# Two-pass dense products, later shifted S5 states and inversions in sequence in a hybrid S5 / SSD / DeltaNet layer

## The chip, the cores and the metric

The kernel runs on one core of one Trainium2 chip. The time is the device time of one execution in microseconds (us): the median of three runs before the change is 1144.62 us (1144.04 to 1144.78). One execution was also profiled; all times of single instructions come from it.

The core has a matrix engine (PE, with its weight loads shown apart as PEld), a vector engine (DVE), a scalar engine (ACT), GpSimd (POOL) and SyncE (SP), which here only issues DMAs. Each engine works through its own instructions in the order in which they were written to it; semaphores tie the engines to one another.

## The reference

One inference step of one layer for 384 tokens: 128 context tokens and 256 latent tokens, with D = 1024 channels. Both groups share the weights, and differ in modulation and in where their scans start.

```python
h = _rmsnorm(x, p['norm_g'][0]) * (1.0 + sc1) + sh1
x = x + 0.5 * g1 * _swiglu(h, p['ffn_wi'][0], p['ffn_wo'][0])
h = _rmsnorm(x, p['norm_g'][1]) * (1.0 + sc2) + sh2
mix, states = _mixer_block(h, p, init, grid)
x = x + g2 * mix
h = _rmsnorm(x, p['norm_g'][2]) * (1.0 + sc3) + sh3
x = x + 0.5 * g3 * _swiglu(h, p['ffn_wi'][1], p['ffn_wo'][1])
```

The feed-forward width is 2816. The mixer projects h once (`w_in`) and runs three branches, all in both directions: an S5 diagonal state space model with a gated output, a Mamba-2 SSD scan, and a gated DeltaNet in chunks of 64 tokens, which solves one lower triangular system of 64 rows per chunk, head and direction. The three branch outputs are projected, each is multiplied by the sigmoid of a gate computed from h, and their sum goes through `w_out`. At the end stands a last RMS norm. The outputs are y for both groups and the context's final states.

## The kernel before

**Layout and dense products.** Activations lie with channels on the partitions, in 8 blocks of 128 x 384. Each dense product uses the fp32r form of the matrix engine on split numbers: a value is written as an upper part (the value cast to fp32r) and a lower part (the rest), and the product is upper x upper + upper x lower + lower x upper. `split_w` (L281) gets one weight block ready: SP loads `wraw` (three buffers), ACT casts it to the upper part `whi` (L285), DVE subtracts to give the lower part `wlo` (L286); `whi` and `wlo` have two buffers each. `mm3` (L291) then makes the product of one block into one PSUM tile. For every k it issues three matmuls: `whi` with the upper activation (L294), `whi` with the lower activation (L295), `wlo` with the upper activation (L296). A full block has k = 0..7, so 24 matmuls of 128 x 384; a block of `wbr` has four k and 12 matmuls. Each matmul loads its own weights.

**Stages.** Start and modulation to 50 us; the first feed-forward (`ffn`, FFN 0) to about 345 us, during which DVE also multiplies out the modulation (`ada_rest`, L272) and ACT and DVE make tables for S5; the mixer to about 860 us; the second feed-forward (FFN 1) to 1130 us; the last norm to the end.

**Inside the mixer.** First come the blocks of `w_in` for S5, q, k and v, each followed by a short convolution (`conv`), and for q and k by transposes on PE into a PSUM tile `ps_m` (two buffers), which ACT copies out (`kT`, `qT`, L825). Beside them DVE runs the S5 scan (L830 to L838). `Hc` (L843 to L853) holds the scan's states shifted by one place and is filled by ACT: per part (real, imaginary) eight pieces, small ones that need only constants or the scan's first 16 places, and two large ones (L850, L852). The S5 readout (L979) uses `Hc`. Then the convolutions for the SSD inputs (`xtok`, `bT`, `cT`, `btok`) and the z product (L896 to L898).

**The triangular systems.** `inv16(d)` inverts the 16 x 16 diagonal blocks of all chunks and heads of one direction on DVE, in 15 steps of a product (L953) and a reduction (L955) that depend on each other; it loads its input `U` from `dL` with four DMAs and writes the result (W, and W transposed by POOL, L958) to `dI` with eight DMAs (L961). `inverse(x, d, ps)` then loads `lc`, `Y` and `X` and builds the 64 x 64 inverse by matmuls in `mm64` (L1045). The chunk recurrence of the DeltaNet (`dn_unit`) and the SSD work follow; this sequence is called the chain below.

**Dense work beside the chain.** A generator `gates()` yields after each piece of dense work: the gates (blocks 22 and up of `w_in`) and the first two branch products. `weave` advances several generators in turn, and `every(n, g, steps)` takes one piece of dense work at every n-th turn. After the chain: `og` (the DeltaNet's output gate), br(2) with its sum `mab` (POOL, L1289), then `og` times the normed output `oacc` (L1298), split into `odh` (ACT, L1300) and `odl` (POOL, L1301), br(3), the gated sums, and `w_out`.

**What sets the order.** The code gives a program order, and the scheduler of the tile framework (`schedule_with_timeline_sim=True`) reorders each engine's instructions by its own model of when they are ready. So an edit in one place can move instructions on every engine.

Of the kernel before, what the change touches and what calls it, by code (L numbers as in the profile page):

```python
# [10 lines left out]
F32 = mybir.dt.float32  # L11
# [9 lines left out]
P = 128  # L21
D = 1024
KD = 8
T = 384
# [117 lines left out]
def tile_hybrid(ctx: ExitStack, tc: tile.TileContext, a, o):  # L142
# [148 lines left out]
    def mm3(pt, w, xh, xl, k0, nk, start, stop):  # L291
        hi, lo = w
        for k in range(nk):
            PE.matmul(pt, hi[:, k, :], xh[k0 + k], start=start and k == 0, stop=False)  # L294
            PE.matmul(pt, hi[:, k, :], xl[k0 + k], start=False, stop=False)  # L295
            last_mm[0] = PE.matmul(pt, lo[:, k, :], xh[k0 + k], start=False, stop=stop and k == nk - 1).ins  # L296
# [95 lines left out]
    def ffn(f, xv, hh, hl, fill, rb=None, done=None, early=(), fill2=None):  # L392
# [5 lines left out]
        for part in range(2):  # L398
            gh, gl = blocks("gh", NH, FR), blocks("gl", NH, FR)
            for j in range(NH):  # L400
# [3 lines left out]
                for w, pt in enumerate((pa, pb)):  # L404
                    mm3(pt, early.pop(0) if early else split_w(a["wi"][f, m, w], KD), hh, hl, 0, KD, True, True)
# [22 lines left out]
            for m in range(KD):  # L428
                py = psd.tile([P, T], F32, name="ps_d", tag="ps_d")
                for k0, nk in ((0, 6), (6, 5)):  # L430
                    w = split_w(a["wo"][f, m, :, part * NH + k0:part * NH + k0 + nk], nk)
                    mm3(py, w, gh, gl, k0, nk, k0 == 0, k0 != 0)
# [182 lines left out]
    def dense_in(blk, hh, hl, tw=T, ps=psD):  # L615
        pt = ps([P, tw])
        mm3(pt, split_w(a["win"][blk], KD), hh, hl, 0, KD, True, True)
# [83 lines left out]
    def mixer(es, xv, acc, xh, xl, sc):  # L701
# [139 lines left out]
        nc.sync.dma_start(out=o["s5"], in_=hfin)  # L841
        Hc = []
# [11 lines left out]


        xtok = mp.tile([P, 3, 8, 64], F32, name="xtok")
        for m in range(4):
            raw = conv(wk, next(urs), dense_in(4 + m, hh, hl), m, sv["cb"][:, m:m + 1])
            pt = transposes([raw[:, X3[x]] for x in range(3)])
            S.copy(xtok.rearrange("p x h c -> p x (h c)")[:, :, m * P:m * P + P], pt)  # L860
        bT, cT = mp.tile([P, T], F32, name="bT"), mp.tile([P, T], F32, name="cT")
        conv(wk, next(urs), dense_in(8, hh, hl), 4, sv["cb"][:, 4:5], bT)
        conv(wk, next(urs), dense_in(9, hh, hl), 5, sv["cb"][:, 5:6], cT)
        btok = mp.tile([P, 3, P], F32, name="btok")
        S.copy(btok, transposes([bT[:, X3[x]] for x in range(3)]))
# [140 lines left out]
        def br(n, m, xh, xl):  # L1006
            pt = psd.tile([P, T], F32, name="ps_d", tag="ps_d")
            mm3(pt, split_w(a["wbr"][m, n], 4), xh, xl, 0, 4, True, True)
# [31 lines left out]
        weave(inv16(0), inv16(1), every(3, dense, 5))  # L1040
# [274 lines left out]
        for m in range(KD):  # L1315
# [3 lines left out]
            mm3(py, split_w(a["wout"][m], KD), mgh, mgl, 0, KD, True, True)  # L1319
# [113 lines left out]
```

## Time and profile before

| | value |
|---|---|
| median of three runs | 1144.62 us |
| profiled execution | 1144.53 us |
| span from first to last instruction | 1142.5 us |
| mean granted PE clock, as share of full | 0.987 |
| PE busy | 1090.7 us (95% of the span) |
| PE's weight loads busy | 1025.8 us (90%) |
| DVE busy | 805.2 us (70%) |
| ACT busy | 472.1 us (41%) |
| POOL busy | 145.1 us (13%) |

The span is 2.0 us shorter than the profiled execution's own time. Busy shares are means over stages with different limits: DVE is at 90% or more in parts of FFN 0 and at about half of that in the second feed-forward. "PE busy" counts matmuls whose ends are modelled, at whichever clock was granted. A wait is put down to the semaphore that came last, so the engine named as the releaser is the one whose result was missing, or, where that engine had long been done, something behind it.

### The profile page before, as it was taken

To read this page: it belongs to the slowest core of one execution; us is meant where nothing else is said; L and a number is where in the kernel's file an instruction comes from. 1 tells how busy PE (TensorE), PEld (TensorE's weight loads), DVE (VectorE), ACT (ScalarE), POOL (GpSimd) and SP (SyncE) were. 2 spreads that over 40 slices of the span, in tenths; PEclk is the share of its full clock that TensorE was granted. 3 is DMA by queue.
4 is the path that set the end of the run, shared out by engine and by line. 5 is a ranking of instruction groups with operands and counts; after the bars stand their busy time and mean duration, and the time that the engine had idled before them with its cause. 6 is when DMAs were issued, how large, how long until landed. Compare 5 with 4: busy or idle time off the path is not lost.

```text
span 1142.5 us, 19011 instructions
## 1 busy us (share of the span) xinstructions
PE 1090.7 (95%) x7192; PEld 1025.8 (90%) x7192; DVE 805.2 (70%) x1652; ACT 472.1 (41%) x871; POOL 145.1 (13%) x135
## 2 busy tenths in 40 slices
PE   5999999999899999899899999999999999999996
PEld 2699899999899999799788888999899999999996
DVE  5699988899967759745554567786866974455554
ACT  5354323333355666743333232243444342334341
POOL 0000000000000100036172563116200000000000
PEclk9999999999999999899999999999999999999998
DMA  9787777576574653268646434456745634544342
GB/s 357 281 265 234 226 232 247 178 225 197 147 262 152 158 171 114 74 189 254 182 144 181 116 105 118 141 158 200 247 142 166 205 112 126 147 115 125 106 127 81
DMA packets 106731, 200.29 MB, mean 175 GB/s; under 512 B 34960, under 2 KB 60816, under 8 KB 106384
## 3 DMA queue, kind: packets, MB, share of 16 engines
q1 hardware_dynamic: 104336, 195.94, 55.7%
q10 hardware_dynamic: 2304, 3.15, 0.8%
q8 instruction: 56, 0.92, 0.3%
q14 instruction: 35, 0.29, 0.1%
HBM read 175.56 MB, written 23.49 MB: 174 GB/s over the span
## 4 chain that ended last, share of the span: by engine, by line
PE 78%; DVE 11%; ACT 3%; issue 3%; DMA 3%; SPq 1%; POOL 1%; DVEq 0%; ACTq 0%; POOLq 0%
PE ps_d L296 21%; PE ps_d L294 21%; PE ps_d L295 20%; DVE wlo L286 3%; ACT whi L285 1%; PE ps_s L979 1%; PE ps_c L1045 1%; PE ps_s L789 1%; PE ps_m L876 1%; PE ps_d L244 1%; DVE cv L687 1%; PE ps_s L1045 1%; DMA cb<-in_condr_dram 1%; DMA wraw<-in_wo_dram 1%; PE ps_m L222 1%
## 5 line engine op out<-in xcount | busy, mean ns | idle before, releaser
L285 ACT CAST whi<-wraw 128x1024 fp32r<-128x1024 f32 (+3 forms) x247 | 228.0, 924 | 450.5 <-PE ps_d L295 300.2
L286 DVE TENSOR_TENSOR wlo<-wraw,whi 128x1024 fp32r<-128x1024 f32 (+3 forms) x247 | 275.1, 1114 | 132.2 <-ACT whi L285 130.2
L294 PE MATMUL ps_d<-hh,whi 128*128 128x384 f32 x696 | 239.4, 345 | 9.9 <-ACT whi L285 6.7
L296 PE MATMUL ps_d<-hh,wlo 128*128 128x384 f32 x696 | 240.2, 346 | 1.3 <-DVE wlo L286 1.1
L295 PE MATMUL ps_d<-hl,whi 128*128 128x384 f32 x696 | 238.3, 343 | 0.9 <-DVE hl L382 0.9
L294 PEld LDWEIGHTS ps_d<-hh,whi 128*128 128x128 f32 x696 | 132.1, 190 | 18.8 <-ACT whi L285 9.9
L296 PEld LDWEIGHTS ps_d<-hh,wlo 128*128 128x128 f32 x696 | 132.2, 190 | 7.5 <-DVE wlo L286 4.1
L295 PEld LDWEIGHTS ps_d<-hl,whi 128*128 128x128 f32 x696 | 132.3, 190 | 3.5 <-DVE hl L382 2.2
L296 PE MATMUL ps_d<-gh,wlo 128*128 128x384 f32 x352 | 119.4, 340 | 3.7 <-DVE wlo L286 3.6
L296 PE MATMUL ps_d<-xh,wlo 128*128 128x386 f32 x352 | 119.7, 340 | 0.9 <-DVE wlo L286 0.9
L294 PE MATMUL ps_d<-gh,whi 128*128 128x384 f32 x352 | 119.0, 338 | 1.5 <-ACT whi L285 1.5
L294 PE MATMUL ps_d<-xh,whi 128*128 128x386 f32 x352 | 119.6, 340 | 0.0
L295 PE MATMUL ps_d<-xl,whi 128*128 128x386 f32 x352 | 119.4, 339 | 0.0
L295 PE MATMUL ps_d<-gl,whi 128*128 128x384 f32 x352 | 118.6, 337 | 0.0
L272 DVE SCALAR_TENSOR_TENSOR ajunk<-araw,cb 128x1024 bf16<-128x1024 f32 x80 | 97.4, 1218 | 2.6 <-ACT cb L264 2.6
L296 PEld LDWEIGHTS ps_d<-gh,wlo 128*128 128x128 f32 x352 | 66.0, 188 | 6.4 <-DVE wlo L286 5.6
L294 PEld LDWEIGHTS ps_d<-gh,whi 128*128 128x128 f32 x352 | 66.1, 188 | 2.7 <-ACT whi L285 2.5
L296 PEld LDWEIGHTS ps_d<-xh,wlo 128*128 128x128 f32 x352 | 66.2, 188 | 1.8 <-DVE wlo L286 1.8
L295 PEld LDWEIGHTS ps_d<-xl,whi 128*128 128x128 f32 x352 | 66.6, 189 | 0.0
L294 PEld LDWEIGHTS ps_d<-xh,whi 128*128 128x128 f32 x352 | 66.2, 188 | 0.0
L295 PEld LDWEIGHTS ps_d<-gl,whi 128*128 128x128 f32 x352 | 66.1, 188 | 0.0
L874 POOL TENSOR_TENSOR Atri<-smalls,dahl 128x512 fp32r<-128x512 f32 x36 | 40.8, 1150 | 61.2 <-DVE dahl L772 53.7
(464 smaller groups left out, 1736.2 us busy)
## 6 DMA issues: line engine op xcount, KB each, us to landing
wraw<-in_wi_dram SPq DMA_DIRECT2D x88, 512.0 KB
araw<-in_ada_dram SPq DMA_DIRECT2D x56, 512.0 KB
wraw<-in_win_dram SPq DMA_DIRECT2D x50, 512.0 KB
wraw<-in_wo_dram SPq DMA_DIRECT2D x32, 384.0 KB
wraw<-in_wo_dram SPq DMA_DIRECT2D x32, 320.0 KB
wraw<-in_ada_dram SPq DMA_DIRECT2D x16, 512.0 KB
wraw<-in_wbr_dram SPq DMA_DIRECT2D x32, 256.0 KB
re<-dM SPq DMA_DIRECT2D x24, 192.0 KB
```

What stands on the lines that cost most here:

```text
L222: PE.matmul(pt[32 * g:32 * g + 32, :], c32[:, k, :], raw[:, j, :], start=q < 2, stop=q >= 2, tile_position=(0, 32 * g))
L244: PE.matmul(pt[32 * g:32 * g + 32, :], c32[:, 4 * h + g, :], raw[:, g, :], start=h == 0, stop=h == 1, tile_position=(0, 32 * g))
L272: V.scalar_tensor_tensor(junk, raw, 1.0, cb[:, e], op0=ALU.mult, op1=ALU.mult, accum_out=t[:, b, e:e + 1])
L285: S.copy(hi, raw)
L286: V.tensor_tensor(lo, raw, hi.bitcast(F32), op=ALU.subtract)
L294: PE.matmul(pt, hi[:, k, :], xh[k0 + k], start=start and k == 0, stop=False)
L295: PE.matmul(pt, hi[:, k, :], xl[k0 + k], start=False, stop=False)
L296: last_mm[0] = PE.matmul(pt, lo[:, k, :], xh[k0 + k], start=False, stop=stop and k == nk - 1).ins
L687: V.scalar_tensor_tensor(rows(cv), ur[:, :, tap:tap + 64], w[:, tap:tap + 1], rows(cv), op0=ALU.mult, op1=ALU.add)
L789: PE.matmul(pt[:, ri, g], sw[:, ri, g], UU[:, 4 * b + g], start=True, stop=True)
L874: G.tensor_tensor(A, bc(INCL[d], [P, 4, P], 1), bc(dahl[:, w, x, 12 * d + c0:12 * d + c0 + 4], [P, 4, P], 2), op=ALU.mult)
L1045: PE.matmul(dst[r_, h], lh[r_, h], rh[r_, h] if len(rh.shape) == 3 else rh[r_], start=True, stop=True)
```

## The change

Three edits, made together.

1. `mm3` issues its matmuls in two passes: first all products with `whi` (L297, L298), for every k, then all products with `wlo` (L305). With `late=True` it keeps the old order, with the lower product as L303. That is set for some first blocks of a stage: the first three m of a feed-forward's first part, the second half of the first `wo` block, block 14 of `w_in`, m = 0 of each branch product and of `w_out`.
2. The `Hc` block is written behind the SSD convolutions instead of ahead of them.
3. The two 16 x 16 inversions run one after the other, each woven with three pieces of dense work at every fifth turn, where before both were woven together with five pieces at every third turn.

Line numbers behind `mm3` grow by 9 to 11: the qT copy is L835, the `Hc` pieces L869 to L874, L953/L955/L961 become L963/L965/L971, L1045 becomes L1056, L1298/L1300/L1301 become L1309/L1311/L1312, L1289 becomes L1300.

```diff
-    def mm3(pt, w, xh, xl, k0, nk, start, stop):
+    def mm3(pt, w, xh, xl, k0, nk, start, stop, late=False):
+
+
         hi, lo = w
-        for k in range(nk):
+
+        def upper(k):
             PE.matmul(pt, hi[:, k, :], xh[k0 + k], start=start and k == 0, stop=False)
             PE.matmul(pt, hi[:, k, :], xl[k0 + k], start=False, stop=False)
+
+        for k in range(nk):
+            upper(k)
+            if late:
+                last_mm[0] = PE.matmul(pt, lo[:, k, :], xh[k0 + k], start=False, stop=stop and k == nk - 1).ins
+        for k in range(0 if late else nk):
             last_mm[0] = PE.matmul(pt, lo[:, k, :], xh[k0 + k], start=False, stop=stop and k == nk - 1).ins
...
-                    mm3(pt, early.pop(0) if early else split_w(a["wi"][f, m, w], KD), hh, hl, 0, KD, True, True)
+                    mm3(pt, early.pop(0) if early else split_w(a["wi"][f, m, w], KD), hh, hl, 0, KD, True, True,
+                        late=part == 0 and m < 3)
...
-                    mm3(py, w, gh, gl, k0, nk, k0 == 0, k0 != 0)
+                    mm3(py, w, gh, gl, k0, nk, k0 == 0, k0 != 0, late=m == 0 and k0 > 0)
...
-        mm3(pt, split_w(a["win"][blk], KD), hh, hl, 0, KD, True, True)
+        mm3(pt, split_w(a["win"][blk], KD), hh, hl, 0, KD, True, True, late=blk == 14)
...
         nc.sync.dma_start(out=o["s5"], in_=hfin)
+
+        xtok = mp.tile([P, 3, 8, 64], F32, name="xtok")
...
+        btok = mp.tile([P, 3, P], F32, name="btok")
+        S.copy(btok, transposes([bT[:, X3[x]] for x in range(3)]))
+
         Hc = []
         for ri in range(2):
             hc = big("Hc", (32, 48))
...
             Hc.append(hc)
-
-
-        xtok = mp.tile([P, 3, 8, 64], F32, name="xtok")
...
-        btok = mp.tile([P, 3, P], F32, name="btok")
-        S.copy(btok, transposes([bT[:, X3[x]] for x in range(3)]))
...
-            mm3(pt, split_w(a["wbr"][m, n], 4), xh, xl, 0, 4, True, True)
+            mm3(pt, split_w(a["wbr"][m, n], 4), xh, xl, 0, 4, True, True, late=m == 0)
...
-        weave(inv16(0), inv16(1), every(3, dense, 5))
+        for d in range(2):
+            weave(inv16(d), every(5, dense, 3))
...
-            mm3(py, split_w(a["wout"][m], KD), mgh, mgl, 0, KD, True, True)
+            mm3(py, split_w(a["wout"][m], KD), mgh, mgl, 0, KD, True, True, late=m == 0)
```

The left-out lines of the two moved blocks are unchanged.

**PE around the transposes of q.** `qtok` is q ahead of its transposes, `cv` the convolved SSD input; the number behind `ps_d` names a dense block. Before:

```order
L296 MATMUL ps_d_4905<-hh_3682,wlo_4909 128x384
L695 MATMUL ps_m_4546<-ident_76,qtok_3839 128x128 x4
L695 MATMUL ps_m_4553<-ident_76,qtok_3839 128x128 x4
L695 MATMUL ps_m_4560<-ident_76,qtok_3839 128x128 x4
L695 MATMUL ps_m_4766<-ident_76,cv_4758 128x128 x3
L695 MATMUL ps_m_4810<-ident_76,cv_4802 128x128 x3
L294 MATMUL ps_d_4944<-hh_3681,whi_4947 128x384
L295 MATMUL ps_d_4944<-hl_3683,whi_4947 128x384
```

Now:

```order
L297 MATMUL ps_d_4841<-hh_3682,whi_4844 128x384
L298 MATMUL ps_d_4841<-hl_3684,whi_4844 128x384
L705 MATMUL ps_m_4546<-ident_76,qtok_3839 128x128 x4
L705 MATMUL ps_m_4553<-ident_76,qtok_3839 128x128 x4
L305 MATMUL ps_d_4841<-hh_3681,wlo_4845 128x384 x4
L305 MATMUL ps_d_4841<-hh_3682,wlo_4845 128x384 x4
L297 MATMUL ps_d_4887<-hh_3681,whi_4890 128x384
```

The transposes of q and of `cv` stood in one row between two dense blocks; now two sets of q stand behind the upper pass of a block with its lower pass behind them, and the third set stands 24 matmuls further on, behind the next block's upper pass. On ACT the twelve small `Hc` pieces stand around the three qT copies in both versions; the four large ones, ahead of the next weight cast before, now stand behind the `btok` copy.

**SP's queue around the inversions.** `W_5538` and its three companions are the inversions' results, `U_5537` and the like their inputs. Before:

```order
L948 DMA U_5547<-dL 24x16x16 x4
L283 DMA wraw<-in_win_dram 128x1024 x4
L1317 DMA xo<-dX 128x384 x2
L242 DMA wraw<-in_ada_dram 128x1024 x2
L961 DMA dI<-W_5538 24x16x16 x4
L961 DMA dI<-W_5847 24x16x16 x4
L961 DMA dI<-W_5548 24x16x16 x4
L961 DMA dI<-W_5857 24x16x16 x4
L1051 DMA lc<-dL 128x4x64
L1058 DMA Y<-dI 128x4x64
L1060 DMA X_5893<-dI 128x4x64
```

Now:

```order
L971 DMA dI<-W_5538 24x16x16 x4
L971 DMA dI<-W_5712 24x16x16 x4
L958 DMA U_5722<-dL 24x16x16 x4
L242 DMA wraw<-in_ada_dram 128x1024
L283 DMA wraw<-in_win_dram 128x1024 x4
L242 DMA wraw<-in_ada_dram 128x1024 x2
L971 DMA dI<-W_5723 24x16x16 x4
L971 DMA dI<-W_5891 24x16x16 x4
L1062 DMA lc<-dL 128x4x64
L1069 DMA Y<-dI 128x4x64
L1071 DMA X_5927<-dI 128x4x64
```

The sixteen writes of `dI` stood in one row; now eight stand behind the first inversion, then the second one's loads and seven loads of dense weights, then the other eight. On PE the first matmul of L1045 stood behind 2352 dense matmuls (those of `mm3` and the z product) and now stands behind 2448 of them, which is four blocks of 24.

**PE and POOL at the end of the chain.** The last transposes of `oacc`, and the dense blocks behind them; `ps_d_8491` is the first block of br(3). PE before:

```order
L294 MATMUL ps_d_8225<-hh_3682,whi_8228 128x384
L695 MATMUL ps_s_8010<-ident_76,oacc_5867 128x128 x4
L295 MATMUL ps_d_8225<-hl_3684,whi_8228 128x384
L296 MATMUL ps_d_8225<-hh_3682,wlo_8229 128x384
L294 MATMUL ps_d_8225<-hh_3682,whi_8228 128x384
L295 MATMUL ps_d_8225<-hl_3684,whi_8228 128x384
L296 MATMUL ps_d_8225<-hh_3682,wlo_8229 128x384
L294 MATMUL ps_d_8225<-hh_3682,whi_8228 128x384
L295 MATMUL ps_d_8225<-hl_3684,whi_8228 128x384
L296 MATMUL ps_d_8225<-hh_3682,wlo_8229 128x384
L294 MATMUL ps_d_8275<-ysh_8259,whi_8278 128x384
L295 MATMUL ps_d_8275<-ysl_8260,whi_8278 128x384
```

PE now:

```order
L298 MATMUL ps_d_8425<-ysl_8260,whi_8428 128x384
L705 MATMUL ps_s_8031<-ident_76,oacc_5901 128x128 x4
L305 MATMUL ps_d_8425<-ysh_8259,wlo_8429 128x384 x4
L297 MATMUL ps_d_8450<-ysh_8259,whi_8453 128x384
L298 MATMUL ps_d_8450<-ysl_8260,whi_8453 128x384
L297 MATMUL ps_d_8450<-ysh_8259,whi_8453 128x384
L298 MATMUL ps_d_8450<-ysl_8260,whi_8453 128x384
L297 MATMUL ps_d_8450<-ysh_8259,whi_8453 128x384
L298 MATMUL ps_d_8450<-ysl_8260,whi_8453 128x384
L297 MATMUL ps_d_8450<-ysh_8259,whi_8453 128x384
L298 MATMUL ps_d_8450<-ysl_8260,whi_8453 128x384
L305 MATMUL ps_d_8450<-ysh_8259,wlo_8454 128x384 x4
L297 MATMUL ps_d_8491<-odh_8120,whi_8494 128x384
```

POOL before:

```order
L1289 TENSOR_TENSOR mab<-mab,re 128x384 x5
L1301 TENSOR_TENSOR odl<-og,odh 128x384 x4
L1289 TENSOR_TENSOR mab<-mab,re 128x384 x3
L1306 TENSOR_TENSOR re<-re,mab 128x384 x8
```

POOL now:

```order
L1300 TENSOR_TENSOR mab<-mab,re 128x384 x7
L1312 TENSOR_TENSOR odl<-og,odh 128x384 x3
L1300 TENSOR_TENSOR mab<-mab,re 128x384
L1312 TENSOR_TENSOR odl<-og,odh 128x384
L1317 TENSOR_TENSOR re<-re,mab 128x384 x8
```

Br(3) begins behind 3096 dense matmuls in both versions; the last transposes of `oacc` stood behind 2992 and now stand behind 3080 of them, so 104 dense matmuls lay between and now 16. The first two blocks of br(3) now run into each other, and on POOL seven of the eight `mab` sums stand ahead of the first `odl`, where five stood.

## Rows read from the trace of the kernel before

**Rows 1.** Page of before: busy time by engine, then the weight preparation's groups by cost.

```profile
PE 1090.7 (95%) x7192; PEld 1025.8 (90%) x7192; DVE 805.2 (70%) x1652; ACT 472.1 (41%) x871; POOL 145.1 (13%) x135
...
L285 ACT CAST whi<-wraw 128x1024 fp32r<-128x1024 f32 (+3 forms) x247 | 228.0, 924 | 450.5 <-PE ps_d L295 300.2
L286 DVE TENSOR_TENSOR wlo<-wraw,whi 128x1024 fp32r<-128x1024 f32 (+3 forms) x247 | 275.1, 1114 | 132.2 <-ACT whi L285 130.2
```

**Rows 2.** PE's waits: engine line waited for: us in total, times, longest us.

```profile
PE ps_d L294 <- ACT whi L285: 8.5, 13, 1.1
PE ps_d L296 <- DVE wlo L286: 6.9, 12, 1.4
PE ps_s L1045 <- DMA X<-dI: 4.4, 1, 4.4
PE ps_m L695 <- ACT qT L825: 4.3, 3, 1.9
```

**Rows 3.** Windows: stretch, length, busy us of PE, PEld, DVE, ACT, POOL, PEclk, DMA, GB/s.

```profile
50.00:350.00 300.00, 290.22 (x1876) 280.27 (x1875) 263.22 (x449) 114.45 (x184) 2.31 (x4) 1.00 0.69 217
350.00:465.00 115.00, 111.45 (x697) 108.65 (x696) 90.65 (x224) 77.79 (x216) 5.40 (x4) 0.99 0.50 143
466.00:473.40 7.40, 3.09 (x19) 1.98 (x17) 6.13 (x20) 7.26 (x19) 0.95 (x1) 0.82 0.31 97
473.40:477.40 4.00, 3.98 (x12) 3.99 (x13) 3.90 (x11) 2.82 (x7) 0.00 (x0) 0.50 0.00 0
566.40:571.30 4.90, 0.58 (x7) 0.10 (x6) 0.00 (x0) 0.86 (x2) 1.09 (x1) 0.83 0.84 209
571.30:576.50 5.20, 4.56 (x52) 3.77 (x53) 1.66 (x2) 2.46 (x3) 0.00 (x0) 0.50 0.93 301
577.00:797.00 220.00, 219.86 (x1787) 196.52 (x1787) 146.13 (x283) 71.14 (x130) 92.53 (x80) 1.00 0.47 140
797.00:1131.00 334.00, 330.49 (x1867) 327.05 (x1866) 206.87 (x386) 131.20 (x202) 10.41 (x9) 1.00 0.48 143
```

**Rows 4.** Timeline of ACT, 465 to 480 us: start, duration, instruction [idle before it].

```profile
469.49 0.56 ACT L825 COPY qT<-ps_m 128x512 f32<-128x512 f32 x1
...
470.59 0.59 ACT L849 COPY Hc<-aT 64x480 f32<-64x480 f32 x1
...
471.80 0.59 ACT L825 COPY qT<-ps_m 128x512 f32<-128x512 f32 x1
...
478.44 1.02 ACT L850 COPY Hc<-aT 64x992 f32<-64x992 f32 x1 [1.55 <-DVE aT L838]
```

**Rows 5.** Timelines of SP's queue, POOL and ACT, 550 to 580 us.

```profile
557.55 8.67 SPq L961 DMA_DIRECT2D dI<-W  x16
...
557.59 2.47 POOL L958 COPY W<-W 96x256 f32<-96x256 f32 x2 [15.71 <-DMA wraw<-in_ada_dram]
...
567.28 0.50 SPq L1060 DMA_DIRECT2D X<-dI  x1
...
573.61 1.04 ACT L285 CAST whi<-wraw 128x1024 fp32r<-128x1024 f32 x1 [0.73 <-DMA wraw<-in_win_dram]
```

**Rows 6.** Groups of the 16x16 inversions by line: xcount | busy us, mean ns.

```profile
L953 DVE TENSOR_TENSOR T<-U,W 96x1 f32<-96x1 f32 (+14 forms) x30 | 7.9, 295 | 0.0
...
L955 DVE TENSOR_REDUCE W<-T 96x1 f32<-96x1 f32 (+14 forms) x30 | 6.1, 231 | 0.0
```

**Rows 7.** Timelines of PE, DVE, ACT and POOL, 772 to 800 us.

```profile
774.45 0.60 PE L695 MATMUL ps_s<-ident,oacc 128*128 128x128 f32 x4
...
775.71 1.68 DVE L1298 SCALAR_TENSOR_TENSOR og<-oacc,hdng,og 128x384 f32<-128x384 f32 x3 [2.22 <-ACT oacc L1234]
...
787.77 1.75 ACT L1300 CAST odh<-og 128x384 fp32r<-128x384 f32 x4
...
788.06 1.42 POOL L1289 TENSOR_TENSOR mab<-mab,re 128x384 f32<-128x384 f32 x1 [0.70 <-DVE mab L1288]
789.42 4.85 POOL L1301 TENSOR_TENSOR odl<-og,odh 128x384 fp32r<-128x384 f32 x4
```

More of the change, by code (lines that the diff above doesn't have):

```diff
@@ L841, in mixer @@
         nc.sync.dma_start(out=o["s5"], in_=hfin)
+        xtok = mp.tile([P, 3, 8, 64], F32, name="xtok")
+        for m in range(4):
+            raw = conv(wk, next(urs), dense_in(4 + m, hh, hl), m, sv["cb"][:, m:m + 1])
+            pt = transposes([raw[:, X3[x]] for x in range(3)])
+            S.copy(xtok.rearrange("p x h c -> p x (h c)")[:, :, m * P:m * P + P], pt)
+        bT, cT = mp.tile([P, T], F32, name="bT"), mp.tile([P, T], F32, name="cT")
+        conv(wk, next(urs), dense_in(8, hh, hl), 4, sv["cb"][:, 4:5], bT)
+        conv(wk, next(urs), dense_in(9, hh, hl), 5, sv["cb"][:, 5:6], cT)
+        btok = mp.tile([P, 3, P], F32, name="btok")
+        S.copy(btok, transposes([bT[:, X3[x]] for x in range(3)]))
         Hc = []
@@ L853, in mixer @@
             Hc.append(hc)
-        xtok = mp.tile([P, 3, 8, 64], F32, name="xtok")
[L857 to L863, printed above, removed]
-        btok = mp.tile([P, 3, P], F32, name="btok")
-        S.copy(btok, transposes([bT[:, X3[x]] for x in range(3)]))
         def segments(x, c0, ps):
```

## The prediction

> **What bounds the kernel now.** I read the page first, then the list of PE's waits, then windows cut at those waits, then the timelines of the stretches that stood out.
>
> The page [rows 1]: PE is busy 95% of the span. ACT's casts `whi` (L285) wait for PE on balance (300.2 us behind the hl matmuls, L295), so over the whole kernel the weight preparation is ahead of PE. The change adds and removes no matmul; a gain can only come out of PE's idle time (1142.5 - 1090.7 = 51.8 us) and out of stretches at half clock.
>
> The windows [rows 3] say where that idle time lies. FFN 0 (50 to 350 us) has 300 - 290.22 = 9.8 us; the head of the mixer (350 to 465) 115 - 111.45 = 3.6; the stretch around the qT copies (466 to 473.4) 7.4 - 3.09 = 4.3; the stretch ahead of the first block inverses (566.4 to 571.3) 4.9 - 0.58 = 4.3, and 0.6 in the one behind it; 577 to 797 only 0.1; 797 to 1131 3.5. Nearly all the rest lies in the first 50 us and the last 11, which the change leaves alone: the instruction order on PE is the same there.
>
> The waits [rows 2] give the causes: 8.5 us for `whi`, 6.9 for `wlo`, 4.4 for one X block that comes by DMA, 4.3 in three waits for ACT's qT copies. And two waits cost more than their idle time [rows 3]: after the qT gap the granted clock is 0.50 for 4.0 us, after the X gap for 5.2 us, which is the 1.2 GHz level; elsewhere in these windows it is near 1.00, the 2.4 GHz level.
>
> **Part A and B: two passes.** In before, `whi` and `wlo` of a 24-matmul block are both free only when the block ends, and `wlo` of the next block is needed at its third matmul. A matmul takes 0.177 us (330.49 us for 1867, [rows 3]), so a block takes 4.2 us. In two passes `whi` is free after 16 of 24 matmuls, 1.4 us earlier, and `wlo` is needed only after 16 matmuls, 2.5 us later than at the third. Cast plus subtraction take 0.92 + 1.11 us in the mean [rows 1], the full-size ones 1.04 to 1.05 [rows 5]. The twelve `wlo` waits have a longest of 1.4 us, the thirteen `whi` waits of 1.1 [rows 2]: each single one is smaller than the slack it gets, if the preparation is only late and not short of throughput.
>
> In FFN 0 that condition is half met. DVE is busy 263.22 of 300 us there [rows 3], so it has 37 us in hand, but it also runs the ada products between the subtractions, and where it is full the delay accumulates past any slack. Of 9.8 us I let 5.5 go (bounds: 3, if only the waits that follow a single late cast go; 9.8, if all). In the head of the mixer ACT (77.8 of 115) and DVE (90.7) are not full, but the blocks there are followed by convolutions that need DVE too: 1 of 3.6 goes (0 to 3). For FFN 1 and the rest (797 to 1131) I take nothing (0 to 2): its idle stretches lie at br(3)/wout, which the third part disturbs. Sum: -6.5. The cost of the order itself I take as zero: the number of weight loads and matmuls is the same, L294 and L295 load the same `whi` one after the other in both versions.
>
> **Part C: shifted states later.** PE's transposes of q need a PSUM buffer that only ACT's qT copies free, and in before these copies stand between twelve small Hc pieces: the second and third copy come at 469.49 and 471.80, with Hc pieces of 0.59 us ahead of each [rows 4]. PE is idle 4.3 us, and the 12 matmuls in the 4.0 us at half clock would take 12 x 0.177 = 2.1 at full: 1.9 us more. Together 6.2. The order of the changed kernel does not show the small pieces gone from there: only the four large pieces (1.02 us each, in before behind the scan at 478.44) stand behind the btok copy. What changes on PE is that the qT transposes no longer stand in one row with the convolution's transposes, but two sets of q behind one upper pass, with 8 lower matmuls (1.4 us) and the next block's upper pass (2.8 us) behind them, and the third set behind that. So the copies can be as slow as before, and dense work covers them. I take 4.5 of 6.2 (bounds 1, if the same wait comes back at the last transposes because DVE, busy 6.13 of 7.4 us, is late with the lower parts; 6.2). The large pieces behind the copies delay only the S5 readout, which waited 0.4 us for them: nothing, since z products lie between.
>
> **Part D: inversions in sequence.** Both inversions need 7.9 + 6.1 = 14.0 us of DVE [rows 6], 7.0 each. In before all sixteen dI writes go out in one row, 8.67 us on SP's queue, X is issued at 567.28, and the weight loads stand behind it, so that the next cast starts at 573.61 [rows 5]. PE idles 4.3 + 0.6 us and then runs at half clock for 5.2 us, of which I count 1.6 as loss (half of the 3.2 us that are dense or chain matmuls at that level, an estimate): 6.5 in all. In after half of the writes go out after the first inversion, so only eight, 4.3 us, stand between the second one's end and X, and seven weight loads stand between the two. The whole stage gets longer: 7.0 + 1.24 (POOL's transposed copy, half of 2.47, [rows 5]) + 4.3 + some 4 for the second U load + 7.0 + 1.24 + 4.3 + some 5 for lc, Y, X = 34 us, plus the subtractions that lie in between, against 29 now; but four more dense blocks, 16.7 us, stand ahead of the first L1045. X is then in time by some us. What is late next are the weights: SP stands in front of dI(0) and dI(1) for up to 7 us each with three raw buffers and two split ones filled. That is cover for about five blocks (21 us), but they are not always full. I leave 3 us of stall and take -3.5 (bounds -6.5 and +6.8, two dry stretches like the one now).
>
> **Part E: the end of the chain.** The dense blocks put ahead of the chain are missing behind it. In before the last transposes of oacc run at 774.45; from there 104 dense matmuls (18 us) stand ahead of the first use of odh, and odl (four by POOL, 4.85 us in all) is done in time [rows 7]: PE idles 0.1 us. In after 16 dense matmuls (2.8 us) stand between. From the transposes: 1.3 us to the first og (775.71), 0.55 for og and 0.44 for the cast give 2.3; POOL then has a mab sum (1.42) ahead, four odl of 1.21 and another mab between them: the last odl is there 9.6 us after the transposes, at best 7. PE comes to the first use after 3.5 us and can do 17 of the two interleaved br(3) blocks' 24 matmuls meanwhile, to 6.5. Stall 9.6 - 6.5 = 3.1, and some clock: +3.5 (bounds 0 and +6).
>
> What a row shows of the clock: in FFN 0 9.8 us of idle in pieces under 1.5 us left it at 1.00, and two gaps whose idle time in one stretch came to 4.3 us cut it to 0.50 [rows 3]. The Trainium skill (TensorE: Matmul & The Clock Gate, "A second HAM failure mode: psum-queue depth-cycling") states that frequent short idle times between matmul groups throttle PE too. By the row E costs 3.1 and little clock; by the rule, with four stalls close together, some 2 us more and the total 1135.6, still inside the forecast's own range below. FFN 0 speaks against the rule, the qT gap, made of three waits, for it.
>
> **Sum.** -5.5 - 1 - 4.5 - 3.5 + 3.5 = -11.0 against the profiled execution, 1144.53 us (span 1142.5 and 2.0 around it), which lies 0.09 under the median 1144.62. So 1133.6 us.
>
> **Rivals.**
> 1. All cover holds: the weights' waits in FFN 0 go almost whole, the qT and X gaps whole, POOL is in time. -9 - 2 - 6.2 - 6 + 0 = -23, 1121.5 us. For it: each wait is smaller than the new slack. Against: DVE's load in FFN 0 and the short cover behind the chain.
> 2. The waits only move. Where DVE or ACT is short of throughput, a later need of `wlo` delays the wait and does not remove it, and the small Hc pieces still stand around the qT copies, so that part two does not do what it says. -2 - 0 - 1 - 1 + 3 = -1, 1143.5 us. For it: the order on ACT, DVE's 6.13 of 7.4 us. Against: the page, where casts wait for PE.
> 3. Slower: the mechanism is SP's queue during the sequential inversions. The weight loads behind the dI writes come late twice, so PE goes dry twice (2 x 6.5 instead of 6.5: +6.5), and since the chain then ends later still against the dense work, br(3) stalls for 6. With -3 - 0 - 4.5 from the rest: +5, 1149.5 us. It decides if the loads of more than five blocks are held for a whole inversion. For it: the queue is in order, and a wraw load stood behind X in before. Against: seven loads between the writes.
>
> **How the numbers follow.** Forecast 0.52 (own range 1128 to 1140), rival 1 0.21, rival 2 0.13, rival 3 0.14. Within 0.2% (2.3 us, about what can be told from no change) is most of rival 2 and a little of rival 3: 0.10; faster: 0.52 + 0.21 + 0.05 of rival 2 = 0.78; slower 0.12. The range 1122 to 1146 leaves out half of rival 1 and most of rival 3, some 0.2.
>
> **What would show it.** A: `whi` and `wlo` waits of FFN 0 down from 9.8 to about 4 us. C: no wait of over 1 us for qT, clock not at 0.50 around it. D: dI writes in two rows of about 4.3 us; the wait for X under 2 us. E: waits for odl of 2 to 4 us in all, at the first br(3) block. Wrong if PE's idle time outside these stretches grows, above all between 577 and 797 in before's count, where it had none; if the waits of FFN 0 are as large as before; or if the half-clock stretches are more than now.

## The result and the profile after

The changed kernel took 1133.13 us in the median of four runs (1129.45 to 1136.45), against 1144.61 us: a ratio of 0.9898, 95% interval 0.9883 to 0.9912. The forecast was 1133.6. The total is therefore right to half a microsecond. Its terms are not: the experiments show a gain more than twice as large as forecast, and a loss of about 14 us that was forecast as nothing. That the two leave the predicted sum is luck.

The profiled run of after is the slowest of its four: span 1134.3 us, time 1136.45 (before: 1142.5 and 1144.53). Its page, in the columns of [rows 1]:

```profile
PE 1089.4 (96%) x7192; PEld 1031.2 (91%) x7192; DVE 805.1 (71%) x1652; ACT 478.7 (42%) x873; POOL 145.7 (13%) x135
...
L285 ACT CAST whi<-wraw 128x1024 fp32r<-128x1024 f32 (+3 forms) x247 | 227.8, 924 | 383.0 <-PE ps_d L298 214.2
L286 DVE TENSOR_TENSOR wlo<-wraw,whi 128x1024 fp32r<-128x1024 f32 (+3 forms) x247 | 268.4, 1092 | 78.2 <-ACT whi L285 55.8
```

PE, DVE and POOL run the same number of instructions as before, ACT two more (873 against 871). ACT's casts still wait for PE (383.0 us before them, 214.2 of it for L298, the second matmul of the upper part). The subtractions cost nearly the same (1092 ns against 1114), but DVE waits 55.8 us for casts ahead of them instead of 130.2. PE's waits, as in [rows 2]:

```profile
PE ps_d L297 <- ACT whi L285: 10.0, 9, 1.8
PE ps_d L297 <- DVE sr L315: 3.4, 1, 3.4
...
PE ps_d L298 <- POOL odl L1312: 2.0, 4, 0.8
...
PE ps_d L297 <- ACT odh L1311: 1.0, 1, 1.0
...
PE ps_s L303 <- DVE wlo L286: 0.5, 1, 0.5
PE ps_s L1056 <- DMA X<-dI: 0.3, 1, 0.3
```

The twelve `wlo` waits of [rows 2] are gone (the 0.5 us left, at 61 us in a block that keeps the old order, stood in before too); the qT waits (4.3 us) are gone, and the wait for X is 0.3 us instead of 4.4. New are 3.4 us in one piece and 3.0 us for `odh` and `odl`, all at the end of the chain.

To place them, I cut both traces where the first matmul of a stage starts. Table of times between such starts, us in the span (the experiments are described below):

| stage | before | after | e1 | e3 | e4 | e9 |
|---|---|---|---|---|---|---|
| start to first mixer block (first `xh`) | 343.8 | 336.4 | 336.6 | 343.4 | 334.7 | 334.5 |
| to first z product (head of the mixer) | 136.0 | 130.2 | 130.2 | 136.2 | 124.8 | 125.6 |
| to first wout matmul (chain) | 332.6 | 338.5 | 329.5 | 328.4 | 328.6 | 324.5 |
| to last matmul of FFN 1 | 316.9 | 316.1 | 314.2 | 316.0 | 314.1 | 314.2 |
| rest of the span | 13.1 | 13.1 | 13.2 | 12.4 | 12.7 | 12.4 |
| span | 1142.5 | 1134.3 | 1123.7 | 1136.4 | 1114.9 | 1111.2 |

After against before: -7.4, -5.8, +5.8, -0.8, 0.0. The chain got slower. Windows of before cut at these starts (columns as in [rows 3]):

```profile
50.00:343.80 293.80, 284.02 (x1841) 274.07 (x1840) 260.12 (x443) 112.28 (x180) 2.31 (x4) 1.00 0.69 217
343.80:479.80 136.00, 128.13 (x781) 124.15 (x780) 105.57 (x265) 91.42 (x247) 6.35 (x5) 0.96 0.48 138
479.80:760.00 280.20, 274.80 (x2327) 242.55 (x2326) 171.42 (x376) 99.51 (x176) 108.73 (x97) 0.99 0.52 154
760.00:793.50 33.50, 33.36 (x192) 33.01 (x191) 23.78 (x47) 13.68 (x25) 10.98 (x9) 1.00 0.64 201
```

and of after:

```profile
50.00:336.40 286.40, 281.17 (x1846) 275.35 (x1845) 257.74 (x442) 113.27 (x180) 2.31 (x4) 1.00 0.71 225
336.40:466.60 130.20, 127.72 (x777) 125.41 (x778) 99.61 (x252) 93.48 (x248) 6.05 (x5) 0.96 0.51 145
466.60:757.00 290.40, 286.06 (x2395) 254.66 (x2394) 185.70 (x390) 106.44 (x186) 107.67 (x97) 0.99 0.51 154
757.00:790.00 33.00, 27.41 (x143) 25.76 (x142) 23.40 (x50) 9.84 (x17) 13.29 (x12) 0.90 0.61 193
769.60:776.30 6.70, 5.85 (x19) 5.88 (x19) 6.34 (x16) 0.62 (x1) 3.10 (x4) 0.51 0.74 240
386.60:392.20 5.60, 5.60 (x26) 5.60 (x26) 2.37 (x3) 4.80 (x19) 0.00 (x0) 0.54 0.50 169
```

The 33 us around the end of the chain hold 5.6 us of PE idle (before 0.1) and 6.7 us at half clock. There 19 matmuls start 0.32 us apart instead of 0.175, 2.8 us more. Idle and clock make 8.4 us; a fourth wait for `odl`, 0.76 us at 791.24, lies behind this window. This is the stage that the change spoils. What PE waited for is read from its timeline, DVE's and SP's queue's (start, duration, instruction [idle before <- releaser]); PE:

```profile
770.45 0.66 PE L297 MATMUL ps_d<-ysh,whi 128*128 128x384 f32 x1 [3.42 <-DVE sr L315]
...
785.24 0.62 PE L297 MATMUL ps_d<-odh,whi 128*128 128x384 f32 x2 [0.99 <-ACT odh L1311]
786.61 0.44 PE L298 MATMUL ps_d<-odl,whi 128*128 128x384 f32 x1 [0.76 <-POOL odl L1312]
```

DVE:

```profile
769.75 0.55 DVE L1299 SCALAR_TENSOR_TENSOR mab<-re,ps_d 128x384 f32<-128x384 f32 x1 [1.58 <-DMA re<-dM]
```

SP's queue:

```profile
539.37 4.80 SPq L971 DMA_DIRECT2D dI<-W  x8
...
563.18 5.65 SPq L971 DMA_DIRECT2D dI<-W  x8
...
569.88 0.50 SPq L1071 DMA_DIRECT2D X<-dI  x1
...
738.28 26.45 SPq L283 DMA_DIRECT2D wraw<-in_wbr_dram  x7
764.84 2.74 SPq L1281 DMA_DIRECT2D re<-dM  x6
```

Read them from the bottom. Seven weight loads, each waiting for DVE to be done with a raw buffer, hold SP's queue from 738.28 for 26.45 us. Behind them stand the loads of `re`, the gates that the br(2) products are multiplied with. They go out at 764.84, the data is there 4.9 us later, DVE's `mab` (769.75) frees the PSUM buffer, and PE, dry for 3.42 us, starts at 770.45. The releaser printed (`sr`) is a neighbour on DVE; `mab` is what ended the wait. DVE had stood 1.58 us of PE's 3.42 for the DMA there. For 1.1 us before that it was still busy, in order, with a weight subtraction and the norm of the last output (L314 to L317) that stand ahead of `mab`; the last 0.7 us are `mab` itself and the way to PE. In before the same loads went out at 761.23, with the first br(2) matmul at 776.28, 15 us behind them; in after that matmul comes at 759.24, ahead of them.

### The profile page after: what moved, and what is told of

Same layout as the page of the kernel before. It is cut to its first block, busy times and chain, and to the rows that moved or that the text cites. A ratio compares the mean times of both kernels' runs of the same rounds, so it can differ in the third digit from the quotient of the medians.

```text
span 1134.3 us, 19013 instructions
## 1 busy us (share of the span) xinstructions
PE 1089.4 (96%) x7192; PEld 1031.2 (91%) x7192; DVE 805.1 (71%) x1652; ACT 478.7 (42%) x873; POOL 145.7 (13%) x135
## 4 chain that ended last, share of the span: by engine, by line
PE 79%; DMA 9%; DVE 5%; ACT 4%; issue 1%; POOL 1%; SPq 1%; ACTq 0%; DVEq 0%; POOLq 0%
PE ps_d L297 22%; PE ps_d L298 21%; PE ps_d L305 19%; DMA wraw<-in_win_dram 4%; PE ps_d L303 1%; ACT whi L285 1%; DVE wlo L286 1%; PE ps_c L1056 1%; DMA wraw<-in_wi_dram 1%; PE ps_m L886 1%; DMA wraw<-in_wo_dram 1%; PE ps_s L799 1%; PE ps_s L1056 1%; PE ps_m L705 1%; PE ps_d L244 1%
## 5 line engine op out<-in xcount | busy, mean ns | idle before, releaser
L285 ACT CAST whi<-wraw 128x1024 fp32r<-128x1024 f32 (+3 forms) x247 | 227.8, 924 | 383.0 <-PE ps_d L298 214.2
L286 DVE TENSOR_TENSOR wlo<-wraw,whi 128x1024 fp32r<-128x1024 f32 (+3 forms) x247 | 268.4, 1092 | 78.2 <-ACT whi L285 55.8
L297 PE MATMUL ps_d<-hh,whi 128*128 128x384 f32 x696 | 241.2, 348 | 6.9 <-ACT whi L285 4.1
L298 PE MATMUL ps_d<-hl,whi 128*128 128x384 f32 x696 | 240.4, 345 | 1.6 <-DVE hl L391 1.6
L297 PEld LDWEIGHTS ps_d<-hh,whi 128*128 128x128 f32 x696 | 133.6, 192 | 15.2 <-ACT whi L285 7.2
L298 PEld LDWEIGHTS ps_d<-hl,whi 128*128 128x128 f32 x696 | 134.4, 193 | 3.9 <-DVE hl L391 3.2
L305 PE MATMUL ps_d<-hh,wlo 128*128 128x384 f32 x664 | 132.6, 339 | 0.0
L297 PE MATMUL ps_d<-gh,whi 128*128 128x384 f32 x352 | 118.8, 338 | 3.1 <-ACT whi L285 3.0
L297 PE MATMUL ps_d<-xh,whi 128*128 128x386 f32 x352 | 119.8, 341 | 1.7 <-ACT whi L285 1.7
L298 PE MATMUL ps_d<-xl,whi 128*128 128x386 f32 x352 | 119.3, 339 | 0.0
L298 PE MATMUL ps_d<-gl,whi 128*128 128x384 f32 x352 | 118.5, 337 | 0.0
L305 PEld LDWEIGHTS ps_d<-hh,wlo 128*128 128x128 f32 x664 | 116.2, 188 | 0.6 <-issue 0.4
L297 PEld LDWEIGHTS ps_d<-gh,whi 128*128 128x128 f32 x352 | 66.1, 188 | 4.4 <-ACT whi L285 4.4
L297 PEld LDWEIGHTS ps_d<-xh,whi 128*128 128x128 f32 x352 | 66.6, 189 | 2.0 <-ACT whi L285 2.0
L298 PEld LDWEIGHTS ps_d<-xl,whi 128*128 128x128 f32 x352 | 66.4, 189 | 0.0
L298 PEld LDWEIGHTS ps_d<-gl,whi 128*128 128x128 f32 x352 | 66.1, 188 | 0.2 <-issue 0.2
L444 DVE SCALAR_TENSOR_TENSOR x<-ps_d,gate,x 128x128 f32<-128x128 f32 x64 | 23.9, 412 | 58.3 <-PE ps_d L305 50.4
L305 PE MATMUL ps_d<-gh,wlo 128*128 128x384 f32 x332 | 65.0, 339 | 0.0
L305 PE MATMUL ps_d<-xh,wlo 128*128 128x386 f32 x328 | 64.5, 338 | 0.0
L305 PEld LDWEIGHTS ps_d<-gh,wlo 128*128 128x128 f32 x332 | 58.3, 188 | 0.6 <-issue 0.6
L305 PEld LDWEIGHTS ps_d<-xh,wlo 128*128 128x128 f32 x328 | 58.4, 189 | 0.0
```

The costliest lines, as they stand in the source:

```text
L285: S.copy(hi, raw)
L286: V.tensor_tensor(lo, raw, hi.bitcast(F32), op=ALU.subtract)
L444: last = V.scalar_tensor_tensor(xv[m][:, s0:s1], py[:, s0:s1], gate[:, m, e:e + 1], xv[m][:, s0:s1], op0=ALU.mult, op1=ALU.add)
```

## The experiments

Twelve kernels ran; each ratio is to before, measured on the same chip (medians 1144.64, 1145.0 and 1144.79 in the three sets).

**e1, two passes alone.** `mm3` and its `late` flags as in the change, the other two parts as before.

> The two passes alone, everything else as in the kernel before. My theory: the two passes are the whole gain of the change (waits for whi and wlo in the first feed-forward down from 9.8 to about 4 us, the qT gap of 4.3 us with its 4 us at half clock gone), and the end of the chain keeps its cover of about 104 dense matmuls, so there is no stall at br(2) and br(3). The X gap of 4.4 us with its half clock stays. So 1144.6 - 6 - 1 - 6 = about 1131 or less, faster than the changed kernel (1133.1) or equal to it. Rival (the inversions in sequence carry the gain): 1138 to 1140, since the X gap stays. Rival (the parts only work together): above 1140.

1118.98 us (1116.28 to 1126.34), 0.9786 [0.9752, 0.9821]: 26 us faster than before and 14 faster than the whole change, and 12 below what was expected. Its profiled run, 1125.77, is one of its two longest; even so the table shows all four stages gaining (-7.2, -5.8, -3.2, -2.7), although the wait for X is longer than before:

```profile
PE ps_d L297 <- ACT whi L285: 6.1, 6, 1.7
PE ps_s L1055 <- DMA X<-dI: 5.1, 1, 5.1
```

**e2, shifted states alone.** Only the Hc block moved behind btok.

> Only the shifted states are written later; two passes and inversions as in the kernel before. My theory: the matmul order on PE is as before and the small Hc pieces still stand around the qT copies, so nothing moves: 1144.6, within 1.5 us, and the qT gap of about 4.3 us with its half clock is there. Rival (this part removed the qT gap): 1138 to 1140.

1144.14 us (11 runs), 0.9992 [0.9981, 1.0003]: nothing. Nor can there be anything: in the two traces every engine runs the same instructions on the same tiles in the same order, so the scheduler put the moved block back where it was. The qT waits of [rows 2] stand unchanged:

```profile
PE ps_m L695 <- ACT qT L825: 4.3, 3, 1.9
```

**e3, inversions in sequence alone.**

```
-        weave(inv16(0), inv16(1), every(3, dense, 5))
+        for d in range(2):
+            weave(inv16(d), every(5, dense, 3))
```

> Only the inversions run in sequence. The transposes of oacc then stand 70 dense matmuls (12 us) ahead of br(3) instead of 104, and four weight loads instead of one stand ahead of the first reload of re. My theory: the X gap (4.4 us and some half clock) goes in part, the weights are late instead by about 3 us, and the end of the chain gives back 1 to 5: 1142 to 1147. Rival (the sequence is a gain by itself): 1138 or less. Rival (the end of the chain costs as much as in the changed kernel): 1149.

1139.79 us, 0.9956 [0.9941, 0.997]: -4.9 us, more than expected. Most of it lies in the chain (-4.3 of -6.1 between the profiles); PE's list has no wait for X, and none for `odl`, since 70 matmuls, not 16, stand in this order between the last oacc transposes and br(3).

**e4, the change without the sequence.** The edit of e3 undone in the changed kernel.

> The changed kernel with the two inversions interleaved as before; two passes and later shifted states stay. My theory: the stall at the end of the chain (3.4 us behind the reload of re, 2.9 us behind odh and odl, and 6.8 us at half clock) goes, the X gap of 4.4 us with its half clock comes back in place of the 3.2 us of the changed kernel: 1126 to 1129, faster than the changed kernel by 4 to 7. Rival (the sequence is a gain, as the prediction took it: -3.5 + 3.5 = 0 or better): 1133 to 1137.

1119.06 us (1116.38 to 1120.83), 0.9765 [0.9743, 0.9787]. So the part that gains 4.9 us alone costs 14 us on top of the two passes (1133.13 - 1119.06; the runs of the two kernels don't overlap). The gain expected from leaving it out was 4 to 7 us. And e4 is not apart from e1: ACT, DVE, POOL and SP run in the same order in both, and PE differs only in the order of some 64 x 64 matmuls of the inverses. So the large `Hc` pieces stand behind the `btok` copy because of the two passes, and not because the block was moved. Its windows, cut at its own starts:

```profile
50.00:334.60 284.60, 280.50 (x1844) 275.02 (x1843) 257.41 (x442) 113.62 (x180) 2.31 (x4) 1.00 0.71 226
334.60:459.40 124.80, 122.94 (x777) 120.70 (x778) 98.88 (x251) 93.10 (x249) 6.06 (x5) 1.00 0.53 152
459.40:771.20 311.80, 304.84 (x2519) 275.58 (x2518) 200.17 (x438) 116.42 (x203) 119.40 (x106) 0.99 0.53 160
```

The head holds 1.9 us of idle (before 7.9) and stays at full clock. The chain holds 7.0, of which 4.1 are the wait ahead of the block inverses that the sequence was to remove; yet it is 9.9 us shorter than after's, above all because its end has no gap. 107 matmuls stand between the oacc transposes and br(3), and SP issues the `re` loads 26 us earlier than in after:

```profile
738.86 3.02 SPq L1280 DMA_DIRECT2D re<-dM  x6
742.92 13.00 SPq L283 DMA_DIRECT2D wraw<-in_wbr_dram  x4
```

**e5, the reloads on another queue** (in the changed kernel).

```
-            nc.sync.dma_start(out=t, in_=dM[m, n])
+            (nc.scalar if n < 2 else nc.sync).dma_start(out=t, in_=dM[m, n])
```

> The changed kernel with the sixteen reloads of re for br(2) issued on ACT's queue, no longer behind seven weight loads in SP's queue. My theory: in the changed kernel PE's 3.4 us at the third br(2) block is the reload standing in SP's queue (the first mab product waits 1.6 us for it on DVE, and three PSUM tiles are full). So that wait and most of the 6.8 us at half clock go: 1127 to 1130. Rival (POOL's and DVE's chain to odl sets the end there): the stall moves to br(3), 1132 to 1134.

1134.51 us (1128.59 to 1139.76), 0.9895 [0.9836, 0.9955]: no gain. The edit did not do what it was to do. ACT's queue is in order too, and there the loads came behind a square of the chain's end, later than on SP's queue; PE:

```profile
773.84 0.41 PE L297 MATMUL ps_d<-ysh,whi 128*128 128x384 f32 x1 [2.50 <-DVE sr L321]
```

and ACT:

```profile
770.07 2.85 ACTq L1281 DMA_DIRECT2D re<-dM  x6
```

DVE's row shows the second cause of this wait:

```profile
773.14 0.56 DVE L1299 SCALAR_TENSOR_TENSOR mab<-re,ps_d 128x384 f32<-128x384 f32 x1 [0.72 <-DMA re<-dM]
```

It stood only 0.72 us for `re`; the rest of the 2.50 it worked on the norm ahead of `mab` and on `mab` itself. An earlier reload alone would thus not have ended PE's wait; in after's order it could have saved the 1.58 us that DVE stood for it, and not the rest. No run had the reload early with the rest unchanged.

**e6, the lower part of the output on DVE** (in the changed kernel).

```
-            G.tensor_tensor(odl[m], f, odh[m].bitcast(F32), op=ALU.subtract)
+            V.tensor_tensor(odl[m], f, odh[m].bitcast(F32), op=ALU.subtract)
```

> The changed kernel with odl made by DVE and not by POOL. My theory: the 2.0 us behind odl at br(3) fall to under 1 and the 3.4 us at br(2) stay: 1131 to 1133. Rival (DVE in its order is as late as POOL, with mab products and weight subtractions ahead): no change, 1133 to 1135.

1134.96 us (1128.18 to 1139.42), 0.9906 [0.9876, 0.9936]: no gain. POOL's four waits become one of DVE's of the same 2.0 us, and the wait ahead stays:

```profile
PE ps_d L297 <- DVE sr L315: 2.7, 1, 2.7
PE ps_d L298 <- DVE odl L1312: 2.0, 1, 2.0
```

PE's order is the same in both. Not POOL's pace alone is short, then: with br(3) only 16 matmuls behind the transposes, DVE is as late. Where 36 or more stand between (e10, e9, e4) no wait for `odl` is left.

**e7, the lower pass first** (e4, each two-pass block starting with the `wlo` matmuls). The same two passes, but `wlo` needed first and `whi` free last.

```
+        for k in range(nk):
+            PE.matmul(pt, lo[:, k, :], xh[k0 + k], start=start and k == 0, stop=False)
+        for k in range(nk):
+            last_mm[0] = upper(k, False, stop and k == nk - 1)
```

> The fastest kernel so far (two passes, later shifted states, inversions interleaved, 1119.1) with the two passes exchanged: all products with the lower part first, then those with the upper part. My theory: the gain of the two passes is that the upper part's buffer is free early and that the lower part, which is ready last, is needed late. Both are lost here, the lower part is needed at the first matmul and the upper part's buffer is held to the end: 1140 to 1150, with waits for wlo in the first feed-forward of 10 us or more. Rival (the order is better for PE itself, since matmuls of one pass stand together): 1117 to 1122.

1154.19 us, 1.008 [1.0055, 1.0105]: 35 us behind e4, 9 behind before. One row of PE's waits says why:

```profile
PE ps_d L306 <- DVE wlo L286: 25.8, 28, 3.0
```

**e8, dI written from two queues** (e4, the second inversion's eight writes issued by ACT).

```
-                    nc.sync.dma_start(out=blk(dI[n], d, b4), in_=w[24 * b4:24 * b4 + 24])
+                    (nc.scalar if n else nc.sync).dma_start(out=blk(dI[n], d, b4), in_=w[24 * b4:24 * b4 + 24])
```

> The kernel without the sequence (1119.1) with half of the sixteen dI writes, those of the transposed blocks, on ACT's queue. My theory: the 4 us wait in front of the first inverse is the row of sixteen writes on SP's queue, 8.7 us; with two rows of 4.3 us it falls under 1 us and its 6.8 us at half clock go: 1113 to 1116. Rival (the wait is the landing of the writes and loads, not their issue, or POOL's copy): 1118 to 1120.

1121.25 us (1117.34 to 1121.51), 0.9771 [0.9718, 0.9823]: no gain over e4. The 4.1 us wait becomes 2.7 for X, and casts take part of the rest (`whi` 7.2 us in all against 4.9 in e4).

**e9 and e10, more dense work ahead of the chain, inversions side by side** (e4, with the block inverses held behind the tenth or eleventh dense block).

```
-        weave(inv16(0), inv16(1), every(3, dense, 5))
+        weave(inv16(0), inv16(1), every(1, dense, 10))
+        hold = [last_mm[0]]
...
-                mm64(pp, Lm[:, lvl], X)
+                with tc.issue_after(hold[0]):
+                    mm64(pp, Lm[:, lvl], X)
```

(e10 has 11 for 10.)

> Two passes, later shifted states, inversions interleaved (1119.1), and the first block inverse is held behind one more dense block: 2472 dense matmuls stand ahead of it on PE by the same count that gives 2448 without it and 2544 in the changed kernel; 80 dense matmuls stand between the last transposes of oacc and br(3) (107 without it, 16 in the changed kernel). My theory: dense work is a fixed stock, and what stands ahead of the chain is missing behind it. One block of 4.2 us just covers the 4.1 us wait in front of the first inverse, its 6.8 us at half clock go too, and 80 matmuls (14 us) still cover the end: 1113 to 1116. Rival (the wait moves to the weights, which stand in SP's queue between the dI writes): 1118 to 1121.

> The same with two more dense blocks ahead of the first inverse (2496), and 36 dense matmuls (6.3 us) between the last transposes of oacc and br(3). My theory: nothing more is won ahead of the chain, and the end begins to show: waits for re, odh or odl at br(2) and br(3) of 2 to 4 us in all, 1115 to 1120. Rival (what hurts the changed kernel is not the missing cover but the inversions in sequence themselves): as fast as with one block or faster, and no waits at br(2) and br(3).

e9: 1117.48 us (1113.22 to 1124.13), 0.9766 [0.9739, 0.9792], the lowest median here, though above the range expected. It is not separable from e4, though its chain is 4.1 us shorter in the profile. The wait ahead of the block inverses is down to 0.3 us, but a wait of 2.23 us for a cast takes its place:

```profile
552.76 0.45 PE L297 MATMUL ps_d<-hh,whi 128*128 128x384 f32 x1 [2.23 <-ACT whi L285]
```

e10: 1120.09 us, 0.9786 [0.9769, 0.9803], not separable from e4 either. I expected 2 to 4 us of waits for `re`, `odh` or `odl` at br(2) and br(3) from the missing cover and found none, only 0.7 us for `wlo`; 36 matmuls are cover enough. Its waits lie elsewhere: 2.2 us for POOL's `Lm`, and casts (10.0 us of `whi`).

```profile
PE ps_c L1057 <- POOL Lm L1065: 2.2, 1, 2.2
```

**e11, only the lower pass late** (e4, first all hi-by-`xh`, then per k hi-by-`xl` and lo-by-`xh`). It is to tell early release of `whi` from late need of `wlo`: `whi` is free only one matmul before the block's end, as in before, and `wlo` needed after 9 matmuls (before after 2, e4 after 16).

```
         for k in range(nk):
-            upper(k)
+            PE.matmul(pt, hi[:, k, :], xh[k0 + k], start=start and k == 0, stop=False)
+        for k in range(nk):
+            PE.matmul(pt, hi[:, k, :], xl[k0 + k], start=False, stop=False)
             last_mm[0] = PE.matmul(pt, lo[:, k, :], xh[k0 + k], start=False, stop=stop and k == nk - 1).ins
```

> Two passes, later shifted states, inversions interleaved, but the second pass takes for every k the upper weight with the lower activation and then the lower weight: the lower part is needed only at the 10th of 24 matmuls, and the upper part's buffer is held to the end as in the kernel before. My theory: both halves of the slack count. The waits for wlo go, those for whi stay in part: 1125 to 1135. Rival (only the later need of wlo matters, since ACT waits for PE on balance): 1117 to 1122. Rival (only the early release of whi matters): above 1138.

1128.03 us, 0.9855 [0.984, 0.987]: 17 of the 26 us. Its waits, and its windows cut at the first `xh` and the first z product:

```profile
PE ps_d L306 <- DVE wlo L286: 2.3, 3, 0.9
PE ps_m L706 <- ACT qT L836: 2.1, 1, 2.1
...
50.00:334.80 284.80, 280.69 (x1841) 274.16 (x1840) 259.82 (x443) 111.94 (x181) 2.31 (x4) 1.00 0.71 224
334.80:468.30 133.50, 128.45 (x778) 125.05 (x777) 101.66 (x259) 93.40 (x247) 6.25 (x5) 0.96 0.48 142
```

FFN 0 ends at 334.8 us, as in e4 (334.7): there the later need of `wlo` alone carries the whole gain. The 9 us behind e4 lie in the head (133.5 us against 124.8): 3.2 us more idle, with a qT wait back, and a mean clock of 0.96 against 1.00. Whether they come from the later release of `whi`, from the other order around the transposes or from the clock alone this run does not tell.

**e12, two passes in every block** (e4, the `late` blocks too).

> Two passes, later shifted states, inversions interleaved, and no exceptions: the first blocks of a stage take two passes too. My theory: at these blocks PE waits for the activations' parts one by one or for the first weights, so the exceptions move some 0 to 2 us: 1118 to 1122. Rival (the exceptions carry a gain at each stage's start): above 1123.

1125.47 us (1123.14 to 1126.39), 0.9827 [0.9813, 0.9842], 6.4 us behind e4. The start is 4.2 us longer by the first gated matmul (138.36 us against 134.14), with waits for `hh` of 4.4 us instead of 2.2 and a clock of 0.52 from 53.7 to 57.2 us. Where a new right side comes late, as here, the one-pass block is the better order.

## Why the total was right and its terms were not

**Bound.** "A gain can only come out of PE's idle time and out of stretches at half clock" held, if idle time is counted from start to start: the listed busy time fell too, from 1090.7 us to 1089.4 in after and 1081.0 in e1, with the same 7192 matmuls. The two mechanisms, weights' waits in FFN 0 and the two gaps, were the right ones.

**A, FFN 0: -5.5 forecast, -7.4 measured.** Idle there fell from 9.8 us to 5.2, near the forecast size; but the stage gained more than its idle time. The listed idle undercounts a wait: the 15 FFN 0 waits of before sum to 9.69 us, while the starts of the matmuls around them lie 12.09 us further apart than the usual pitch. So 9.8 was too low a ceiling. The reserve that I took for a full DVE was not called on. At the two largest waits left there, 1.65 us at 302.79 and 1.66 at 336.43, PE waits for a cast, and the cast had waited for its weights to come by DMA; ACT before the first of them:

```profile
301.90 0.83 ACT L285 CAST whi<-wraw 128x768 fp32r<-128x768 f32 x1 [4.93 <-DMA wraw<-in_wo_dram]
```

**B, head: -1 forecast, and C, qT gap: -4.5; together -5.8 measured in after's profile, -11.2 in e4's.** The qT gap and the half clock behind it went whole. The difference between the two profiles is mostly clock: after's head holds half-clock stretches from 387 to 394 and 408 to 411 us, as much in all as before's (372 to 375, which the mean of 0.99 in [rows 3] hid, and 471 to 478), e4's none. The inversions in sequence do not make that difference: after and e4 have the same order of instructions on every engine up to 523 us. I credited C to the moved states only in its heading; its working named the upper passes around the transposes as the cover. e2 and e1 show that the heading was wrong and the working right: the move does nothing, two passes do it.

**FFN 1: 0 forecast, bound 2; -0.8 in after, -2.7 in e1, -2.8 in e4.** Part of the 3.5 us of idle there could go too; without the sequence the gain passed the bound.

**D, inversions: -3.5 forecast.** The wait for X fell to 0.3 us, as said, and dI went out in two rows of 4.80 and 5.65 us against 4.3. But two cast waits of 1.80 and 1.12 us took its place, the first with a half clock behind it; in the windows of the chain up to its end, 290 and 280 us long, idle is 4.3 us against 5.4. In the changed kernel D is thus worth about 1 us of idle time and not 3.5, another term that was too large. As a part alone (e3, -4.9) it came out near its forecast.

**E, end of the chain: +3.5 forecast, bounds 0 to +6; +8.4 measured in its 33 us, 9.2 with the wait behind them.** This is the step that failed. The wait it named is there at its size: 0.99 for `odh` and 1.95 in four for `odl`, 3.0 us against 3.1. What it left out is the queue one stage earlier. I asked only what br(3) needs, and not what br(2), pulled forward to 759 us, needs: `re` from SP's queue, behind seven waiting weight loads, and a `mab` that DVE reaches only behind the chain's last norm. That cost 3.4 us and was followed by the half clock, 2.8 us. Two of the forecast's own signs of being wrong came with it: idle time at br(2), where before had none, and more time at half clock between 50 and 1120 us (some 20 us against 17).

**The sum.** For the whole change against e4, the forecast was -3.5 + 3.5 = 0; measured were 9.9 us in the chain's profile and 14 in the medians. For two passes against before it was -11; measured were -26. Rival 1's sum (1121.5) is near what the change gives without the sequence (1119.06), though its X gap stays there. Rival 3's places (SP's queue, then br(3)) are where a part of it was lost, but at the chain's end and not during the inversions. Of the 9.9 us, 3.7 are idle time (10.7 us in after against 7.0); some 2 are clock, an estimate from what starts at half clock in both traces (29 dense matmuls 0.32 us apart in after; 6 of them and 48 small ones in e4); about 4 are not placed. The profiles themselves lie 19.4 us apart, but 7.1 of that come before 523 us, where both kernels run the same order: after's profile is its longest run, e4's near its shortest. How after's four runs come to spread over 7 us stays open.

## What to carry to other kernels

Where an operand is split in two parts with a buffer each, order the matmuls so that the part prepared last is needed last (in FFN 0 that alone carried the gain) and the part prepared first is released first; with late right sides keep the one-pass order. Dense work put ahead of a serial chain is missing behind it: count the cover that is left, and the loads queued ahead of what the pulled-forward work needs. Test parts of a change alone and in the company of the others: one that gains 5 us alone lost 14 beside another. And look whether the scheduler kept an edit at all: the moved block came out in the old order.

## What the hardware showed beyond the forecast

- The granted clock is hard to foresee from single waits. After a 1.80 us wait at 553.53 us the next 4 us of after ran at 0.61, near the 1.2 GHz level; after a wait of 2.23 us at the same place e9 ran on at 1.00. In after's 386.6 to 392.2 window PE was busy throughout (5.60 of 5.60 us) at 0.54. FFN 0 of before, with 15 waits under 1.5 us, kept 1.00 [rows 3].
- The same order of instructions can get another clock: up to the first z product after and e4 run the same work in the same order on every engine, and the head took 130.2 us at a mean of 0.96 in one and 124.8 at 1.00 in the other.
- Runs of one kernel fall with the clock: after's four took 1136.45, 1133.41, 1132.86 and 1129.45 us at mean granted clocks of 0.982, 0.985, 0.986 and 0.991.
- A wait costs PE more than its listed idle, some 0.16 us each here ((12.09 - 9.69) / 15), and the matmul after the late one starts 0.28 us behind it instead of 0.175.
